# Mix and branch products with the tokens standing still and 512 weight columns moving

## The chip, the cores and the metric

The kernel runs on one core of a Trainium2 chip. The time is device time in microseconds of one execution; lower is better. Three timed runs of the kernel before gave 646.74, 647.31 and 647.63 us, and their median is what the change is compared with.

The engines have short names here. PE is TensorE, which multiplies; PEld is its loading of the operand that stands still. DVE is VectorE, ACT is ScalarE, POOL is GpSimd, and SP starts the loads. A product (one MATMUL) holds a 128x128 block in the array and moves up to 512 columns of the other operand past it. The block that stands still is loaded by an LDWEIGHTS instruction of its own, one for each product.

## The reference

Two layers are computed on 256 tokens of 1024 features. Each layer projects the normed tokens (w_in), runs three attentions (branches a, b and m), and merges the three results with gates that come from a "mix" projection:

```python
    ys = jnp.stack([ya, yb, ym], axis=2)
    up = jnp.einsum('bsnw,nwd->bsnd', ys, w_branch)
    gates = jax.nn.sigmoid(mix.reshape(b, s, N_BRANCH, D_MODEL))
    merged = jnp.sum(gates * up, axis=2)
    return x + jnp.einsum('bsd,de->bse', merged, w_out)
```

The mix projection has 3 x 1024 columns of w_in with 1024 rows each. The branch product has 3 x 512 rows and 1024 columns. The merged matrix, 256 x 1024, goes through w_out. After the second layer the tokens are normed once more and written out.

## The kernel before

All products are in float32, with each operand split in a high and a low part (`split`, lines 101 to 103: ACT rounds the value to `hi`, DVE subtracts to get `lo`). A product of the computation is then three products on the engine (`mm3`, lines 105 to 108: high by high, high by low, low by high).

Weights come in units (`unit`, lines 78 to 90): one load of up to 128x1024 float32 into `raw`, then the split into `whi` and `wlo`. There are four buffers of each, so PE can be at most four units behind the load.

Two helpers do the projections. `rows_first` (line 160) holds 128 tokens still and moves up to 512 weight columns; its result has tokens on partitions. `cols_first` (line 178) holds 128 weight columns still and moves all 256 tokens; its result has the columns on partitions. The queries, keys and values use `rows_first`; the gates and the mix use `cols_first`.

At the end of each layer the merge runs over eight blocks of 128 merged columns. `mixes(j)` (lines 510 to 519) projects block j of the three branches and takes tanh of half of it on ACT. The loop over j (lines 525 to 549) does the branch products of block j, 36 of 256 columns each, into two PSUM banks (`ups`). DVE forms (tanh + 1) * up for the three branches (line 543), POOL adds the three (lines 545 and 546), ACT writes half the sum to `mh[:, j]` (line 547) and DVE the rest to `ml[:, j]` (line 548). Since the columns are on partitions there, `mh` and `ml` are already in the form that `w_out` holds still. `mixes` runs three blocks ahead of the merge.

Then `w_out` multiplies: for k from 0 to 7 it takes block k of `mh` and `ml` against row block k of w_out, 12 products of 512 columns for each k. In the second layer the last three k stand behind the loop, and one bank's columns are cut in two.

A scheduler sets the order of the instructions on each engine when the kernel is built. It moves instructions past one another where the data allow it, and each engine then works off its own list strictly in order. So the mix products stand partly among the attention of branch b, where PE would otherwise wait for softmax.

Of the kernel before, what the change touches and what calls it, by code (L numbers as in the profile page):

```python
# [13 lines left out]
P = 128  # L14
# [11 lines left out]
RAW = 4  # units of weights on their way  # L26
WARM = 10  # products on zeros that wake the tensor engine's clock while the first loads are under way
WS = (64 ** -0.5) * (8 ** -0.5)

# columns of w_in, in groups of 512  # L30
# [4 lines left out]
def trunk(ctx, tc, x, x_t, mem, mem_t, consts, norm_g, gains, w_grp, w_idx, w_mix, w_kv, w_br, w_o, final_g, out):  # L35
# [13 lines left out]
    def two(tag="big"):  # L49
        """a tile for the high and the low parts: [P, 2, 1024]"""  # L50
        return big.tile([P, 2, 1024], F32R, tag="big", name=tag)
# [43 lines left out]
    def load_after(dst, src):  # L95
        """a load that waits for the newest unit, so that it doesn't hold up the units before it"""
        nc.gpsimd.tensor_copy(dst.rearrange("p a b -> p (a b)")[:, 0:1] if len(dst.shape) > 2 else dst[:, 0:1],
                              newest[0][:, 0:1].bitcast(F32))
        nc.sync.dma_start(dst, src)
# [19 lines left out]
    def transpose_to(dst_fn, src, t):  # L119
        """[P, 1024] -> 8 blocks [128, P]; dst_fn(c, psum [P, 4, 128])"""  # L120
# [6 lines left out]
    def rstd_row(rows, rs):  # L127
        """1 / rms of the tokens: on partitions in rs, and in a row, the same on all partitions"""
# [11 lines left out]
    def mem_prep(l, mh, ml, ks):  # L140
        """mem but for 1 / rms, with features on partitions"""
# [18 lines left out]
    def rows_first(wsrc, xh, xl, parts, n, done, ahead=lambda u: None, pools=None, first=False):  # L160
        """tokens on partitions: out[t][:, part] = x @ w, w [P, KC, n]"""
# [16 lines left out]
    def cols_first(wsrc, xh, xl, nt, done, ahead=lambda u: None):  # L178
        """columns on partitions: out[c] = (x @ w).T, w [P, KC, nt * 128]; done(pair of tiles, psum)"""
# [16 lines left out]
    def rope(t, ps, dst, nh):  # L196
        """dst [P, nh, 64] = rope of psum [P, nh, 64]"""
# [11 lines left out]
    def heads_T(qf, dst):  # L209
        """qf[t] [P, 512] -> dst [P, 2, (pair, token)], heads on partitions"""  # L210
# [18 lines left out]
    def values(l, g, hh, hl, name):  # L229
        """[P, token tile, (head, part, 64)]: the high part first for even heads, last for odd ones, so that it  # L230
        meets the rows of y that the head has"""
# [10 lines left out]
    def gate(l, g, hh, hl, s2):  # L242
        """s2 [P, 4, S] = 2 silu(h @ w).T"""
# [6 lines left out]
    def probs(t, nk, tm, nb, scale=-1.0):  # L250
        """softmax rows of scale * tm, whose maximum is -nb"""
# [11 lines left out]
    def pair_scores(p, qT, kT, at):  # L263
        """both heads of a pair, each on its half of the rows and in its own bank: queries of the first tile
        meet the high and the low parts of their 128 keys side by side, those of the second tile all keys"""
# [30 lines left out]
    def attn_out(p, prs, v, y, s2):  # L296
# [13 lines left out]
        for i, pool in enumerate(((psa, "sc"), (pst, "pt"))):  # L310
            # high and low parts of v on rows; the low parts of the second queries' later keys in columns of their own
# [59 lines left out]
    def index_mask(l, hh, hl):  # L371
        """additive masks of the keys that each query picks"""
# [39 lines left out]
        def turn(t, r):  # L412
            """one turn of a query tile: takes the 8 largest that are left, the earlier of equals first"""
# [16 lines left out]
    def normed_first(xT):  # L430
        """of x that is laid out with features on partitions"""
# [23 lines left out]
    for l in range(L):  # L455
# [54 lines left out]
        def mixes(j):  # L510
            """tanh(mix / 2).T of columns j of the branches"""
            mx = wk.tile([P, 3, S], F32, tag="mix", name="mx", bufs=5)

            def done(c, ps):
                n = 2 if c == 0 else 1
                nc.scalar.activation(mx[:, 2 * c:2 * c + n, :], ps[:, :n * S].rearrange("p (a b) -> p a b", b=S),  # L516
                                     AF.Tanh, scale=0.5)
            cols_first(w_mix[l, j], hh, hl, 3, done)
            return mx

# [3 lines left out]
        mxs = [mixes(j) for j in range(3)]  # L524
        for j in range(8):
            if j + 3 < 8:
                mxs.append(mixes(j + 3))
            if j == 4 and l + 1 < L:
                mhl = mem_tiles()
                mem_prep(l + 1, *mhl, range(KC))  # L530
            ups = [bank(pmm, "mm"), bank(pmm, "mm")]
            for u in range(2):
                hi, lo = unit(w_br[l, j, :, u * 6:(u + 1) * 6, :], 768)
                for q in range(6):
                    n, k = divmod(u * 6 + q, 4)
                    o = ups[n // 2][:, (n % 2) * S:(n % 2 + 1) * S]
                    ww = slice(q * P, (q + 1) * P)
                    yy = slice(k * S, (k + 1) * S)
                    mm3(o, hi[:, ww], lo[:, ww], ys[n][:, 0, yy], ys[n][:, 1, yy], k == 0 and n != 1, k == 3)
            mx = mxs[j]  # L540
            mt = [mx[:, n, :] for n in range(3)]
            for n in range(3):
                nc.vector.scalar_tensor_tensor(mt[n], mx[:, n, :], 1.0, ups[n // 2][:, (n % 2) * S:(n % 2 + 1) * S],  # L543
                                               op0=ALU.add, op1=ALU.mult)
            nc.gpsimd.tensor_tensor(mt[0], mt[0], mt[1], op=ALU.add)  # L545
            nc.gpsimd.tensor_tensor(mt[0], mt[0], mt[2], op=ALU.add)  # L546
            nc.scalar.activation(mh[:, j, :], mt[0], AF.Copy, scale=0.5)  # L547
            nc.vector.scalar_tensor_tensor(ml[:, j, :], mt[0], 0.5, mh[:, j, :].bitcast(F32),
                                           op0=ALU.mult, op1=ALU.subtract)
# [124 lines left out]
```

## Time and profile before

| what | value |
|---|---|
| median of three runs | 647.31 us |
| lowest and highest | 646.74 and 647.63 us |
| span of the profiled execution, first to last instruction | 645.5 us |
| PE busy | 632.1 us, 98% of the span, 4446 recorded products |
| DVE busy | 468.8 us, 73% |
| ACT busy | 372.6 us, 58% |
| POOL busy | 121.0 us, 19% |
| read from memory | 106.81 MB, 167 GB/s over the span |

The profile gives the span of its execution as its time; the median of the timed runs lies 1.8 us above it. Busy time says that an engine had at least one instruction in work. Since products overlap in the array (one is recorded for 0.28 to 0.40 us, the next begins 0.12 to 0.23 us later), the price of a product is read from the distance between two starts, not from its recorded length.

### The profile page before, as it was taken

The numbers are of one execution on the slowest core, as the hardware profiler recorded it, in microseconds if no ns is written. First come the engines' busy times: TensorE is split into PE (matmuls) and PEld (weight loads), VectorE is DVE, ScalarE is ACT, GpSimd is POOL, SyncE is SP. The second block draws the span as 40 slices with busy tenths as digits, with TensorE's granted clock in tenths as the row PEclk, the third lists the DMA queues.
The fourth block names the chain that finished last, engine by engine and source line by source line (L and its number), as shares of the span: only waits on it lengthen the run. The fifth ranks groups of instructions, "written<-read, shape, count | busy, mean of one in ns | idle before, by whom it ended". The sixth has DMA issues, their size and how long they took to land.

```text
span 645.5 us, 12071 instructions
## 1 busy us (share of the span) xinstructions
PE 632.1 (98%) x4446; PEld 583.1 (90%) x4446; DVE 468.8 (73%) x1014; ACT 372.6 (58%) x725; POOL 121.0 (19%) x182
## 2 busy tenths in 40 slices
PE   7999999999999999999999999999999999999995
PEld 4989889878999999999889998897898999999984
DVE  5678799778777778557584678987777786755763
ACT  5857655666656756444464656656565766544442
POOL 1303022023102302126010200401210211221422
PEclk9999999999999999999999999999999999999998
DMA  8967454454444456667655745445444445566641
GB/s 298 360 201 233 150 160 141 156 162 137 111 142 124 125 145 198 195 174 221 214 174 135 264 152 164 134 133 170 151 127 133 131 127 148 171 187 184 206 127 65
DMA packets 35051, 108.64 MB, mean 168 GB/s; under 512 B 4016, under 2 KB 4016, under 8 KB 34992
## 3 DMA queue, kind: packets, MB, share of 16 engines
q1 hardware_dynamic: 34704, 107.35, 54.7%
q8 instruction: 35, 0.57, 0.4%
q10 hardware_dynamic: 288, 0.52, 0.2%
q14 instruction: 24, 0.20, 0.1%
HBM read 106.81 MB, written 1.05 MB: 167 GB/s over the span
## 4 chain that ended last, share of the span: by engine, by line
PE 93%; DMA 3%; DVE 2%; ACT 1%; issue 1%; SPq 0%; POOLq 0%; POOL 0%; ACTq 0%; DVEq 0%
PE mm L106 24%; PE mm L108 24%; PE mm L107 24%; PE sc L271 2%; PE sc L108 2%; PE sc L106 2%; PE sc L107 2%; DMA raw<-in_w_kv 2%; PE sc L275 2%; PE pt L216 1%; PE pt L301 1%; DMA xT<-in_x_t 1%; PE pt L106 1%; PE pt L108 1%; PE pt L107 1%; PE pt L303 1%
## 5 line engine op out<-in xcount | busy, mean ns | idle before, releaser
L103 DVE TENSOR_TENSOR wlo<-raw,whi 128x1024 fp32r<-128x1024 f32 (+3 forms) x225 | 246.9, 1099 | 99.5 <-ACT whi L102 98.5
L102 ACT CAST whi<-raw 128x1024 fp32r<-128x1024 f32 (+3 forms) x225 | 208.1, 927 | 130.3 <-PE mm L107 52.0
L107 PE MATMUL mm<-hl,whi 128*128 128x256 f32 x640 | 183.4, 287 | 0.0
L106 PE MATMUL mm<-hh,whi 128*128 128x256 f32 x640 | 182.9, 286 | 0.0
L108 PE MATMUL mm<-hh,wlo 128*128 128x256 f32 x640 | 182.6, 286 | 0.0
L106 PEld LDWEIGHTS mm<-hh,whi 128*128 128x128 f32 x640 | 122.6, 192 | 1.3
L107 PEld LDWEIGHTS mm<-hl,whi 128*128 128x128 f32 x640 | 122.6, 192 | 0.8
L108 PEld LDWEIGHTS mm<-hh,wlo 128*128 128x128 f32 x640 | 122.4, 192 | 0.7
L108 PE MATMUL mm<-whi,hl 128*128 128x512 f32 (+1 forms) x224 | 84.8, 381 | 1.4 <-DVE hl L103 1.4
L107 PE MATMUL mm<-wlo,hh 128*128 128x512 f32 (+1 forms) x224 | 85.7, 384 | 0.0
L106 PE MATMUL mm<-whi,hh 128*128 128x512 f32 (+1 forms) x224 | 84.2, 380 | 0.0
L260 POOL TENSOR_SCALAR pr<-pr,rinv 128x256 f32<-128x256 f32 (+1 forms) x80 | 40.7, 526 | 183.6 <-DVE rinv L258 175.9
L108 PEld LDWEIGHTS mm<-whi,hl 128*128 128x128 f32 x224 | 42.1, 189 | 8.3 <-DVE hl L103 1.7
L107 PEld LDWEIGHTS mm<-wlo,hh 128*128 128x128 f32 x224 | 42.2, 189 | 7.0
L106 PEld LDWEIGHTS mm<-whi,hh 128*128 128x128 f32 x224 | 41.8, 188 | 7.3
L255 ACT ACTIVATE pr<-tm,nb 128x128 f32<-128x128 f32 (+1 forms) x80 | 36.5, 459 | 9.1 <-DVE nb L291 9.0
L545 POOL TENSOR_TENSOR mx<-mx 128x256 f32<-128x256 f32 x16 | 21.3, 1334 | 102.8 <-DVE mx L543 102.8
L207 POOL TENSOR_TENSOR qf<-rt,rt 128x128 f32<-128x128 f32 (+2 forms) x24 | 16.8, 704 | 121.2 <-DVE rt L206 121.2
L546 POOL TENSOR_TENSOR mx<-mx 128x256 f32<-128x256 f32 x16 | 23.1, 1446 | 12.6 <-DVE mx L543 11.5
L543 DVE SCALAR_TENSOR_TENSOR mx<-mx,mm 128x256 f32<-128x256 f32 x48 | 18.6, 415 | 6.6 <-PE mm L108 6.5
L516 ACT ACTIVATE mx<-mm 128x512 f32<-128x512 f32 (+1 forms) x32 | 15.7, 490 | 12.9 <-PE mm L108 12.9
L547 ACT ACTIVATE mgh<-mx 128x256 fp32r<-128x256 f32 x16 | 6.7, 418 | 25.5 <-POOL mx L546 25.5
(252 smaller groups left out, 1220.9 us busy)
## 6 DMA issues: line engine op xcount, KB each, us to landing
raw<-in_w_grp SPq DMA_DIRECT2D x80, 512.0 KB, 3.9
raw<-in_w_mix SPq DMA_DIRECT2D x64, 384.0 KB, 3.2
raw<-in_w_br SPq DMA_DIRECT2D x32, 384.0 KB, 3.4
raw<-in_w_o SPq DMA_DIRECT2D x16, 512.0 KB, 4.4
raw<-in_w_kv SPq DMA_DIRECT2D x15, 512.0 KB, 4.4
raw<-in_w_idx SPq DMA_DIRECT2D x16, 292.0 KB, 3.1
memT<-in_mem_t SPq DMA_DIRECT2D x4, 256.0 KB, 6.0
xr<-in_x SPq DMA_DIRECT2D x2, 512.0 KB, 6.6
```

Of the source, the lines that this page charges most:

```text
L102: nc.scalar.copy(hi, src)
L103: nc.vector.tensor_sub(lo, src, hi.bitcast(F32))
L106: nc.tensor.matmul(o, lh, rh, start=start, stop=False, skip_group_check=True)
L107: nc.tensor.matmul(o, lh, rl, start=False, stop=False, skip_group_check=True)
L108: nc.tensor.matmul(o, ll, rh, start=False, stop=stop, skip_group_check=True)
L207: nc.gpsimd.tensor_tensor(dst[:, :, 0:16], t1[:, :nh], t2[:, :nh], op=ALU.add)
L255: nc.scalar.activation(pr[:, i, :nk], tm[:, i, :nk], AF.Exp, bias=nb[:, i:i + 1], scale=scale, accum_out=rsum[:, i:i + 1])
L260: nc.gpsimd.tensor_scalar(pr[:, i, :nk], pr[:, i, :nk], rinv[:, i:i + 1], 1.0, op0=ALU.mult, op1=ALU.mult)
L516: nc.scalar.activation(mx[:, 2 * c:2 * c + n, :], ps[:, :n * S].rearrange("p (a b) -> p a b", b=S), AF.Tanh, scale=0.5)
L543: nc.vector.scalar_tensor_tensor(mt[n], mx[:, n, :], 1.0, ups[n // 2][:, (n % 2) * S:(n % 2 + 1) * S], op0=ALU.add, op1=ALU.mult)
L545: nc.gpsimd.tensor_tensor(mt[0], mt[0], mt[1], op=ALU.add)
L546: nc.gpsimd.tensor_tensor(mt[0], mt[0], mt[2], op=ALU.add)
```

## The change

The mix projection and the branch products take 512 weight columns at a time with the tokens still, so that their results have tokens on partitions. The merge runs over two halves b of 512 merged columns and three branches n, in six steps instead of eight. `mixes(b, n)` is now a `rows_first` with two banks, one for each 128 tokens, and one tanh for each. `merge(b, n)` does the branch products of one branch, 24 of 512 columns, multiplies them on DVE by (tanh + 1), and from the second branch on adds the result to the first branch's on POOL. After the third branch `merged_T` transposes the 128x512 halves on PE, four 128x128 blocks for each 128 tokens, and ACT and DVE write `mh` and `ml` from the transposed bank. The arrays w_mix and w_br are laid out for this on the host. `w_out` is unchanged.

```diff
-        def mixes(j):
-            """tanh(mix / 2).T of columns j of the branches"""
-            mx = wk.tile([P, 3, S], F32, tag="mix", name="mx", bufs=5)
...
-            cols_first(w_mix[l, j], hh, hl, 3, done)
+        def mixes(b, n):
+
+            mx = wk.tile([P, NT, 512], F32, tag="mix", name="mx", bufs=4)
+            rows_first(w_mix[l, b, n], hh, hl, [(0, 512)], 512,
+                       lambda t, i, ps: nc.scalar.activation(mx[:, t], ps, AF.Tanh, scale=0.5))
             return mx
+
+        def merge(b, n, mx, acc):
+
+            ups = [bank(pmm, "mm") for _ in range(NT)]
+            for u in range(2):
+                hi, lo = unit(w_br[l, b, n, :, 2 * u:2 * u + 2, :], 1024)
+                for q in range(2):
+                    k = 2 * u + q
+                    ww = slice(q * 512, (q + 1) * 512)
+                    for t in range(NT):
+                        yy = slice(k * S + t * P, k * S + (t + 1) * P)
+                        mm3(ups[t], ys[n][:, 0, yy], ys[n][:, 1, yy], hi[:, ww], lo[:, ww], k == 0, k == 3)
+            for t in range(NT):
+                nc.vector.scalar_tensor_tensor(mx[:, t], mx[:, t], 1.0, ups[t], op0=ALU.add, op1=ALU.mult)
+                if n:
+                    nc.gpsimd.tensor_tensor(acc[:, t], acc[:, t], mx[:, t], op=ALU.add)
+
+        def merged_T(b, acc):
+
+            bs = slice(4 * b, 4 * b + 4)
+            for t in range(NT):
+                tt = slice(t * P, (t + 1) * P)
+                pt = bank(pmm, "mm")
+                for i in range(4):
+                    nc.tensor.transpose(pt[:, i * P:(i + 1) * P], acc[:, t, i * P:(i + 1) * P], ident)
+                pt = pt.rearrange("p (a b) -> p a b", b=P)
+                nc.scalar.activation(mh[:, bs, tt], pt, AF.Copy, scale=0.5)
+                nc.vector.scalar_tensor_tensor(ml[:, bs, tt], pt, 0.5, mh[:, bs, tt].bitcast(F32),
+                                               op0=ALU.mult, op1=ALU.subtract)
...
-        mxs = [mixes(j) for j in range(3)]
-        for j in range(8):
-            if j + 3 < 8:
-                mxs.append(mixes(j + 3))
-            if j == 4 and l + 1 < L:
+        todo = [(b, n) for b in range(2) for n in range(3)]
+        mxs = [mixes(*todo[j]) for j in range(3)]
+        for j, (b, n) in enumerate(todo):
+            if j == 3 and l + 1 < L:
                 mhl = mem_tiles()
                 mem_prep(l + 1, *mhl, range(KC))
...
+            merge(b, n, mxs[j], mxs[3 * b])
+            if j + 3 < 6:
+                mxs.append(mixes(*todo[j + 3]))
+            if n == 2:
+                merged_T(b, mxs[3 * b])
```

The names in the rows below: `hh` and `hl` are the normed tokens, `yA`, `yM`, `yB` the branch results, `mm`, `sc` and `pt` PSUM banks, `mx` the tanh and then the gated branches, `mgh` and `mgl` the tiles that the code calls mh and ml, `cst` holds the identity. A line that begins with a minus stands in the list of before alone, one with a plus in that of after alone, one with neither in both.

PE in the first layer, among the last projections of the attention of branch b, where the first mix products stand:

```order
+L107 MATMUL mm<-wlo,hh 128x512
+L108 MATMUL mm<-whi,hl 128x512
+L106 MATMUL mm<-whi,hh 128x512
 L216 MATMUL pt<-cst,qf 128x128 x4
-L107 MATMUL mm<-hl,whi 128x256
 L271 MATMUL sc<-bk,bq 128x256 x4
 L275 MATMUL sc<-bk,bq 128x256 x6
-L108 MATMUL mm<-hh,wlo 128x256
-L106 MATMUL mm<-hh,whi 128x256
```

Each pair of 256-column products there has become one of 512 columns, in which the tokens (`hh`, `hl`) stand still; the attention's own products have stayed where they were among them.

PE at the end of the first layer's merge, before: the branch products run straight into those of w_out.

```order
L106 MATMUL mm<-yB,whi 128x256
L107 MATMUL mm<-yB,whi 128x256
L108 MATMUL mm<-yB,wlo 128x256
L106 MATMUL sc<-whi,mgh 128x512
L107 MATMUL sc<-wlo,mgh 128x512
L108 MATMUL sc<-whi,mgl 128x512
L106 MATMUL pt<-whi,mgh 128x512
```

PE at the same place after, where the products of w_out for k = 2 are under way:

```order
L106 MATMUL pt<-whi,mgh 128x512
L107 MATMUL pt<-wlo,mgh 128x512
L540 MATMUL mm<-cst,mx 128x128 x4
L108 MATMUL pt<-whi,mgl 128x512
L106 MATMUL sc<-whi,mgh 128x512
L540 MATMUL mm<-cst,mx 128x128 x4
L107 MATMUL sc<-wlo,mgh 128x512
```

The transposes of the second half now stand among the w_out products, 26 products behind the last branch product in the first layer (27 in the second), and the second four come two products later (three in the second layer). Those of the first half stand together, eight in a row, behind the last mix product.

DVE at the end of the first layer's merge, after, with the engines that each instruction waits for:

```order
L529 SCALAR_TENSOR_TENSOR mx<-mx,mm 128x512 [waits PE_49,Pool_49]
L103 TENSOR_TENSOR wlo<-raw,whi 128x1024 [waits DMAHW2_49,Activation_49]
L529 SCALAR_TENSOR_TENSOR mx<-mx,mm 128x512 [waits PE_49]
L103 TENSOR_TENSOR wlo<-raw,whi 128x1024 [waits DMAHW3_49,Activation_49]
L103 TENSOR_TENSOR wlo<-raw,whi 128x1024 [waits DMAHW4_49,Activation_49]
L529 SCALAR_TENSOR_TENSOR mx<-mx,mm 128x512 [waits PE_49,Pool_49]
L529 SCALAR_TENSOR_TENSOR mx<-mx,mm 128x512 [waits PE_49]
L103 TENSOR_TENSOR wlo<-raw,whi 128x1024 [waits DMAHW5_49,Activation_49]
```

Before, three half as wide ones stood between two splits there, with the write of `mgl` ahead of them. Now the two multiplications of the last branch stand behind the splits of the first three w_out units, and POOL's last two adds wait for them.

## Rows read from the trace of the kernel before

**Rows 1.** The page: engine, busy us, share of the span, instructions.

```profile
PE 632.1 (98%) x4446; PEld 583.1 (90%) x4446; DVE 468.8 (73%) x1014; ACT 372.6 (58%) x725; POOL 121.0 (19%) x182
```

**Rows 2.** The page: the chain that ended last, by engine.

```profile
PE 93%; DMA 3%; DVE 2%; ACT 1%; issue 1%; SPq 0%; POOLq 0%; POOL 0%; ACTq 0%; DVEq 0%
```

**Rows 3.** Stretches: us, busy PE, PEld, DVE, ACT, POOL, granted clock, DMA, GB/s.

```profile
130.00:140.00 10.00, 10.00 (x54) 7.98 (x54) 8.38 (x24) 6.40 (x17) 3.27 (x8) 1.00 0.54 161
...
240.00:250.00 10.00, 10.00 (x86) 10.00 (x85) 8.59 (x17) 7.72 (x16) 1.32 (x1) 1.00 0.64 193
...
270.00:280.00 10.00, 10.00 (x86) 10.00 (x85) 5.51 (x9) 4.88 (x8) 2.77 (x2) 1.00 0.69 181
...
310.00:320.00 10.00, 10.00 (x46) 8.29 (x45) 4.10 (x4) 4.21 (x4) 0.00 (x0) 1.00 0.70 224
```

**Rows 4.** All waits of PE: who for whom, us, times, longest.

```profile
PE mm L106 <- ACT whi L102: 2.1, 2, 1.2
PE pt L74 <- POOL idle L71: 1.5, 1, 1.5
PE mm L108 <- DVE hl L103: 1.4, 1, 1.4
PE mm L107 <- DVE wlo L103: 0.5, 1, 0.5
```

**Rows 5.** PE, 262 to 282 us, mix and branch products: first, last of 169.

```profile
261.74 0.28 PE L107 MATMUL mm<-yB,whi 128*128 128x256 f32 x1
...
281.90 0.28 PE L107 MATMUL mm<-hl,whi 128*128 128x256 f32 x1
```

**Rows 6.** PE, 306 to 330 us, products of 512 columns: first, last of 107.

```profile
305.82 0.39 PE L108 MATMUL pt<-whi,mgl 128*128 128x512 f32 x1
...
329.85 0.39 PE L106 MATMUL mm<-whi,mh 128*128 128x512 f32 x1
```

**Rows 7.** PE around eight transposes: start us, recorded us, line, operation.

```profile
332.35 0.40 PE L108 MATMUL mm<-whi,ml 128*128 128x512 f32 x1
332.58 1.04 PE L124 MATMUL pt<-cst,h 128*128 128x128 f32 x8
333.37 0.48 PE L106 MATMUL mm<-whi,mh 128*128 128x512 f32 x1
333.69 0.40 PE L107 MATMUL mm<-wlo,mh 128*128 128x512 f32 x1
```

**Rows 8.** Groups by form: line, engine, operation, count, busy us, mean ns, idle before.

```profile
L103 DVE TENSOR_TENSOR wlo<-raw,whi 128x1024 fp32r<-128x1024 f32 x111 | 138.1, 1245 | 49.2 <-ACT whi L102 48.4
...
L102 ACT CAST whi<-raw 128x1024 fp32r<-128x1024 f32 x111 | 116.4, 1050 | 71.0 <-PE mm L108 19.8 <-issue 16.3 <-PE mm L107 10.6
...
L247 DVE SCALAR_TENSOR_TENSOR s<-th,mm 128x512 f32<-128x512 f32 x12 | 8.2, 685 | 1.1 <-ACT th L246 1.0
...
L145 DVE SCALAR_TENSOR_TENSOR ml<-memT,gm,mh 128x256 fp32r<-128x256 f32 x16 | 6.8, 478 | 5.2 <-ACT mh L144 5.2
...
L362 DVE SCALAR_TENSOR_TENSOR pl<-pt,rsm,ph 128x512 fp32r<-128x512 f32 x8 | 5.7, 737 | 0.0
```

**Rows 9.** POOL's adds: count, shortest, median, longest ns, first and last start.

```profile
L545 POOL TENSOR_TENSOR mx<-mx x16: 737/1358/1592, 237.2 to 616.0; 128x256 f32<-128x256 f32 x16
L546 POOL TENSOR_TENSOR mx<-mx x16: 1317/1442/1602, 243.7 to 617.6; 128x256 f32<-128x256 f32 x16
...
L589 POOL TENSOR_TENSOR o<-xr,gb x1: 1276/1276/1276, 637.2 to 637.2; 128x512 f32<-128x512 f32 x1
```

More of the change, by code (lines that the diff above doesn't have):

```diff
@@ L508, in trunk @@
         attend(bq, bk, lambda: values(l, B_V, hh, hl, "bv"), masks, yB, s2[1])
-        def mixes(j):
-            mx = wk.tile([P, 3, S], F32, tag="mix", name="mx", bufs=5)
[L514 to L517, printed above, removed]
-            cols_first(w_mix[l, j], hh, hl, 3, done)
-            return mx
+        def mixes(b, n):
+            mx = wk.tile([P, NT, 512], F32, tag="mix", name="mx", bufs=4)
+            rows_first(w_mix[l, b, n], hh, hl, [(0, 512)], 512,
+                       lambda t, i, ps: nc.scalar.activation(mx[:, t], ps, AF.Tanh, scale=0.5))
+            return mx
+        def merge(b, n, mx, acc):
[23 more added lines that the diff above has]
+                                               op0=ALU.mult, op1=ALU.subtract)
         mh = big.tile([P, KC, S], F32R, tag="big", name="mgh")
@@ L523, in trunk @@
         ys = [yA, yM, yB]
-        mxs = [mixes(j) for j in range(3)]
-        for j in range(8):
-            if j + 3 < 8:
-                mxs.append(mixes(j + 3))
-            if j == 4 and l + 1 < L:
+        todo = [(b, n) for b in range(2) for n in range(3)]
+        mxs = [mixes(*todo[j]) for j in range(3)]
+        for j, (b, n) in enumerate(todo):
+            if j == 3 and l + 1 < L:
                 mhl = mem_tiles()
                 mem_prep(l + 1, *mhl, range(KC))
[L531 to L549, printed above, removed]
+            merge(b, n, mxs[j], mxs[3 * b])
[3 more added lines that the diff above has]
+                merged_T(b, mxs[3 * b])
         last = 3 if l + 1 == L else 0
@@ L645 @@
     order = [0, 2, 1]
-    mix = wr[..., 5704:].reshape(L, P, KC, 3, 8, P)[:, :, :, order]
-    mix = mix.transpose(0, 4, 1, 2, 3, 5).reshape(L, 8, P, KC, 384)
-    br = w_branch[:, order].reshape(L, 3, 4, P, 8, P).transpose(0, 4, 3, 1, 2, 5).reshape(L, 8, P, 12, P)
+    mix = wr[..., 5704:].reshape(L, P, KC, 3, 2, 512)[:, :, :, order].transpose(0, 4, 3, 1, 2, 5)
+    br = w_branch[:, order].reshape(L, 3, 4, P, 2, 512).transpose(0, 4, 1, 3, 2, 5)
     arrays = {
```

## The prediction, made before the changed kernel ran

> **What bounds the kernel now.** I read the page's busy times first, then its chain, then the stretches. PE is busy for 98% of the span while DVE, at 73%, is next [rows 1]. That alone says little, since a product is recorded for longer than it occupies the array. The chain is the better witness: 93% of what ended last is PE's own work [rows 2]. In the stretches PE is busy for the whole 10 us, in the attention (130 to 140 us), in the mix and branch products (240 to 280 us) and in w_out (310 to 320 us), at a granted clock of 1.00, the 2.4 GHz level [rows 3]. All of PE's waits together are 5.5 us, and none is for a gated branch, for POOL's adds or for `mgl` [rows 4]. So in the stage that changes PE is the bound, DVE and ACT have 14 to 51% left, and a change is worth there what it takes from PE's list or adds to it.
>
> **What one product costs.** It is read between starts. In the mix and branch stage 169 products of 256 columns begin between 261.74 and 281.90 us: 20.16 / 168 = 0.1200 us each [rows 5]. In w_out and the memory projection 107 products of 512 columns begin between 305.82 and 329.85 us: 24.03 / 106 = 0.2267 us each [rows 6]. Two narrow products take 0.2400 us, a wide one 0.2267, for the same arithmetic. If each product is a part per column plus a fixed part, the fixed part is 0.0133 us, and the change removes one for each pair. In all 107 the weights move and tokens or merged columns stand still, as in the new products, so the wide price is that of the new form.
>
> **Products removed and added.** Before, one layer has 8 blocks x 24 column tiles (8 row blocks x 3 branches) x 3 = 576 mix products and 8 x 36 = 288 branch products, 864 in all; two layers have 1728 of 256 columns. They go, and 864 of 512 columns come. 1728 x 0.1200 = 207.4 us become 864 x 0.2267 = 195.9 us: 11.5 us less on PE.
>
> At this place a rule speaks against the change. The Trainium skill, "TensorE: Matmul & The Clock Gate", section "Back-to-back issue gap", gives N / 2.4 + 2.5 ns between starts at full clock. An estimate by it would be 109.2 and 215.8 ns, 2.6 ns saved per pair and 2.2 us in all, less than the transposes below cost. The trace does not agree: both prices are higher [rows 5, 6], and the saving per pair is 13.3 ns.
>
> **Transposes added.** Four blocks for each 128 tokens, each half and each layer: 32. Around eight of them the product before starts at 332.35 and the second product after at 333.69 us [rows 7]; of the 1.34 us two normal spacings (0.45) are the products' own, so eight cost 0.89 us, of which 0.10 is the hand-over behind them. Each layer has one group of eight and two of four (half of 0.79 plus 0.10, so 0.49): 2 x (0.89 + 0.98) = 3.7 us on PE.
>
> **Work beside PE.** A unit of 1024 columns takes 1.25 us on DVE and 1.05 on ACT [rows 8] and feeds 12 wide products, 2.72 us of PE, in the mix as in the branches. The same helper feeds the same widths in w_out today, where PE has no hole [rows 3]. So splits and loads stay hidden. The tanh, the gating and the writing of `mgh` and `mgl` become fewer and wider; on an engine with idle time that is worth nothing. Mix products also fill PE among the softmax of branch b. There the narrow ones are replaced by wide ones, as branch a has them today without a hole at 130 to 140 us [rows 3]. I take nothing for that; bounds 0 and 1.5 us, the latter the size that the totals of PE's waits have [rows 4].
>
> **The new wait.** Before, the merged blocks left the branch products one by one, and only the last of eight was young when w_out needed it, seven blocks later. Now the second half's transposes stand in PE's list behind POOL's last adds, and everything behind them on PE waits too. In the first layer 26 w_out products cover that (5.9 us from the last branch product, which I call E), and the second four follow at E + 5.9 + 0.49 + 2 x 0.227 = E + 6.8. In the second layer it is 27, and E + 7.3.
>
> What must be done by then, first layer: from the start of the half's first branch product to E PE has 75 products, 17.0 us. In that time DVE has six splits (7.5 us), two writes of `mgl` (1.5), eight preparations of the next layer's memory (3.8) and six gatings (4.1) [rows 8], 16.9 us; it starts about 1 us late, behind two tanh and a cast on ACT, so its last gating ends near E + 1.1. POOL has four adds in a row, from the first gating of the middle branch (by the same walk E - 4.8). With a for one 128x512 add they end at E - 4.8 + 4a, and PE stands still for 4a - 11.6 us if that is positive. In the second layer the memory is not prepared; the adds start near E - 5.1, and the loss is 4a - 12.4.
>
> No row has this add at this place. The bound below is 1.28 us, the one 128x512 add, at the end where DVE does little [rows 9]. The bound above is twice the longest half-wide add, 2 x 1.60 = 3.20; twice the medians is 2.7 to 2.9. At 2.9 both losses are nil, at 3.20 they are 1.2 and 0.4 us. I take nothing, by the medians, and keep 0 to 1.6 us. After the transposes ACT and DVE need about 0.7 us each per 128 tokens [rows 8], with 19 products (4.3 us) of k = 2 and 3 left on PE in the first layer; that is covered. The first half's transposes have 48 mix products (10.9 us) in front of them, more than a gating and two adds at 3.20. If any of this cover were missing, a whole chain of gating, add, transpose and two writes would cost at most 0.7 + 2 x 3.2 + 0.5 + 1.4 = 9.0 us per layer.
>
> **The sum.** -11.5 + 3.7 + 0 = -7.8 us. The profiled span of 645.5 becomes 637.7. The median lies 1.8 us above that span, so the time is 639.5 us.
>
> **Rivals.**
> - *Part of it is given back* (0.09). The adds take 3.2 us or more, or DVE, which the first layer's second half leaves with hardly any slack, comes late, or PE finds holes among the softmax of branch b. For it: DVE's 16.9 us against PE's 17.0. Against it: PE waited for none of these before [rows 4]. Price 2 to 6.5 us: 641.5 to 646.
> - *The adds become the bound, slower than before* (0.04). One mechanism at one place: POOL's four adds before the second half's transposes. The loss over both layers is 8a - 24.0 us; it eats the gain at a = 4.0, and the kernel is slower by more than 0.2% from a = 4.1. At a = 4.5 it is 12.0 us and the time 651.5. For it: the half-wide add goes from 0.74 to 1.60 us within this kernel [rows 9], so something stretches it up to twofold. Against it: 4.0 would be 2.5 times the longest of the 32.
> - *The change does not do what it says: the wide product saves nothing in this place* (0.03). Then only the transposes are left, +3.7 us, 651.0. Against it: the same form, tokens still and 512 columns, runs in the attention's projections at no visible loss, and 0.2267 is measured in the stage right behind [rows 6]. The rule of the skill named above would give 2.2 us back, -2.2 + 3.7 = +1.5 us, 648.8, a milder form of this rival.
>
> **How the numbers follow.** The forecast, a saving of some 6 to 9 us, has 0.84: 638.5 to 641.5, which are the two unknowns' bounds (1.6 and 1.5 us less than fully added) and half a microsecond of spread, as in the three runs. The range for 8 in 10 reaches a little into the first rival: 638.3 to 643.5. A measurement of this kernel can tell about 0.2%, 1.3 us, from no change, so faster means below 646.0. Forecast and nearly all of the first rival lie there, 0.91; same 0.04; slower 0.05, from the last two rivals with a little of each left in between.
>
> **What would show it.** Right, step by step: starts in the mix and branch products 0.227 us apart; 1728 fewer and 864 + 32 more products; eight transposes taking about 0.8 us; no wait of PE for POOL's adds or only tenths; PE busy through every stretch from 130 us on; 128x512 adds between 1.3 and 3.2 us. Wrong: a wait of PE at the transposes of the second half, several microseconds long, would be the second rival; waits for `whi` and `wlo` in the branch products of the first layer's second half, the first; a spacing near 0.240, the third.

## The result, and the profile after

The changed kernel takes 640.54 us, the median of 4 runs (640.47 to 640.62), against 647.24 us (646.74 to 647.63) for the kernel before on the same chip. The ratio is 0.9896, 95% interval 0.9882 to 0.991: faster by 6.7 us. The forecast was 639.5, so the time lies inside the range, 1.0 us above the forecast. The profiled execution spans 638.7 us (645.5 before).

The page of the kernel after, its engines and its chain, to be read beside [rows 1, 2]:

```profile
PE 626.2 (98%) x3614; PEld 540.2 (85%) x3614; DVE 467.3 (73%) x958; ACT 368.9 (58%) x685; POOL 105.5 (17%) x166
...
PE 94%; DVE 2%; DMA 1%; issue 1%; ACT 0%; POOLq 0%; SPq 0%; POOL 0%; ACTq 0%; DVEq 0%
```

PE has 832 instructions fewer, which is 1728 less 864 less 32. It still makes up nearly the whole chain, so what leaves PE's list leaves the time.

Two of the stretches of [rows 3], after (from and to, length, then busy us and instructions of PE, PEld, DVE, ACT and POOL, granted clock, DMA share, GB/s):

```profile
240.00:250.00 10.00, 10.00 (x50) 8.32 (x49) 5.32 (x7) 5.97 (x10) 0.00 (x0) 1.00 0.59 187
270.00:280.00 10.00, 10.00 (x46) 8.29 (x45) 5.61 (x6) 4.15 (x4) 3.54 (x2) 1.00 0.61 204
```

PE is busy throughout at a granted clock of 1.00, with about half as many products. It is so in the other two stretches too, 130 to 140 and 310 to 320 us. All of its waits, as in [rows 4]:

```profile
PE mm L106 <- ACT whi L102: 1.6, 1, 1.6
PE pt L74 <- POOL idle L71: 1.5, 1, 1.5
PE mm L108 <- DVE hl L103: 1.4, 1, 1.4
PE mm L108 <- DVE wlo L103: 0.2, 1, 0.2
```

None is for POOL's adds, for a gating or for `mgl`, and all four lie before 180 us. The new price of a product, in a run of products with nothing between them (first and last of 23; start us, recorded us, engine, line, operation):

```profile
283.78 0.39 PE L107 MATMUL mm<-wlo,yA 128*128 128x512 f32 x1
...
288.76 0.39 PE L108 MATMUL mm<-whi,yM 128*128 128x512 f32 x1
```

4.98 / 22 = 0.2264 us, the spacing of w_out in [rows 6].

**Where the time came from.** Two marks are the same work in both kernels: the first transpose of branch b's queries, which stands just ahead of what the change touches in the first layer, and the first transpose of the next layer's norm, which stands behind it (its row of before is in [rows 7]). Before, the first mark:

```profile
178.66 0.49 PE L216 MATMUL pt<-cst,qf 128*128 128x128 f32 x3
```

After, both marks:

```profile
178.98 0.49 PE L216 MATMUL pt<-cst,qf 128*128 128x128 f32 x3
...
329.38 0.49 PE L124 MATMUL pt<-cst,h 128*128 128x128 f32 x3
```

From mark to mark it was 153.92 us and is 150.40: 3.52 less. The start is 0.32 later. From the second mark to the last product PE needs 304.75 us before (637.33 - 332.58) and 301.19 after: 3.56 less. 0.32 - 3.52 - 3.56 = -6.76, the 6.8 us between the spans.

The stretch between the marks, by kind of product. Each column sums the distances from one start to the next, so a hand-over is counted with the neighbour in which it falls; each entry is rounded by itself. The last two columns belong to experiments below.

| us between the marks (count) | before | after | e1, 256 | e3, no transposes |
|---|---|---|---|---|
| products of 256 columns | 105.78 (864) | none | 105.63 (864) | none |
| products of 512 columns | 37.20 (163) | 137.14 (595) | 37.43 (163) | 136.80 (595) |
| transposes of the merged matrix | none | 1.50 (16) | 1.50 (16) | none |
| transposes of probabilities (24) | 1.56 | 2.00 | 1.56 | 2.00 |
| transposes of queries and keys (16) | 1.50 | 1.67 | 1.50 | 1.67 |
| probabilities times values (24) | 2.96 | 3.18 | 3.20 | 3.18 |
| scores (40) | 4.92 | 4.90 | 4.92 | 4.90 |
| sum | 153.92 | 150.40 | 155.73 | 148.56 |

### The profile page after: what moved, and what is told of

It is laid out like the page before. It is cut to its first block, busy times and chain, and to the rows that moved or that the text cites. A ratio compares the mean times of both kernels' runs of the same rounds, so it can differ in the third digit from the quotient of the medians.

```text
span 638.7 us, 10185 instructions
## 1 busy us (share of the span) xinstructions
PE 626.2 (98%) x3614; PEld 540.2 (85%) x3614; DVE 467.3 (73%) x958; ACT 368.9 (58%) x685; POOL 105.5 (17%) x166
## 3 DMA queue, kind: packets, MB, share of 16 engines
HBM read 106.81 MB, written 1.05 MB: 169 GB/s over the span
## 4 chain that ended last, share of the span: by engine, by line
PE 94%; DVE 2%; DMA 1%; issue 1%; ACT 0%; POOLq 0%; SPq 0%; POOL 0%; ACTq 0%; DVEq 0%
PE mm L107 25%; PE mm L108 25%; PE mm L106 25%; PE sc L271 2%; PE sc L106 2%; PE sc L107 2%; PE sc L108 2%; PE sc L275 2%; PE pt L216 1%; PE pt L301 1%; PE pt L106 1%; PE pt L107 1%; PE pt L108 1%; DMA raw<-in_w_grp 1%; PE pt L303 1%; DMA memT<-in_mem_t 1%
## 5 line engine op out<-in xcount | busy, mean ns | idle before, releaser
L103 DVE TENSOR_TENSOR wlo<-raw,whi 128x1024 fp32r<-128x1024 f32 (+2 forms) x201 | 246.4, 1229 | 109.9 <-ACT whi L102 108.9
L102 ACT CAST whi<-raw 128x1024 fp32r<-128x1024 f32 (+2 forms) x201 | 204.2, 1018 | 151.5 <-PE mm L108 67.3
L108 PE MATMUL mm<-whi,hl 128*128 128x512 f32 (+2 forms) x416 | 160.3, 387 | 1.4 <-DVE hl L103 1.4
L107 PE MATMUL mm<-wlo,hh 128*128 128x512 f32 (+2 forms) x416 | 160.8, 387 | 0.0
L106 PE MATMUL mm<-whi,hh 128*128 128x512 f32 (+2 forms) x416 | 159.7, 386 | 0.0
L108 PE MATMUL mm<-hh,wlo 128*128 128x256 f32 x256 | 73.3, 287 | 0.2 <-DVE wlo L103 0.2
L107 PE MATMUL mm<-hl,whi 128*128 128x256 f32 x256 | 73.3, 287 | 0.0
L106 PE MATMUL mm<-hh,whi 128*128 128x256 f32 x256 | 72.7, 285 | 0.0
L106 PEld LDWEIGHTS mm<-hh,whi 128*128 128x128 f32 x256 | 48.9, 191 | 0.4
L107 PEld LDWEIGHTS mm<-hl,whi 128*128 128x128 f32 x256 | 48.9, 191 | 0.4
L514 ACT ACTIVATE mx<-mm 128x512 f32<-128x512 f32 x24 | 14.1, 596 | 12.0 <-PE mm L108 11.5
```

The lines of the kernel that those rows point to most:

```text
L102: nc.scalar.copy(hi, src)
L103: nc.vector.tensor_sub(lo, src, hi.bitcast(F32))
L106: nc.tensor.matmul(o, lh, rh, start=start, stop=False, skip_group_check=True)
L107: nc.tensor.matmul(o, lh, rl, start=False, stop=False, skip_group_check=True)
L108: nc.tensor.matmul(o, ll, rh, start=False, stop=stop, skip_group_check=True)
L514: lambda t, i, ps: nc.scalar.activation(mx[:, t], ps, AF.Tanh, scale=0.5))
```

## The experiments

The theory: each product costs a fixed 13.3 ns beside its columns, PE's list is the time, the transposes take their forecast price, and POOL's adds end before PE needs them. The rivals: the gain came from something else in the new arrangement than the width; the transposes or the adds cost a different sum than they seem to. Each ratio below is against the kernel before timed beside the run (medians 647.03 to 647.26 us); differences to the changed kernel go by its 640.54 us, so some 0.2 us of them may be no more than the spread of these medians.

**e9, the changed kernel again.** It gives the noise of a second look. Nothing is edited.

> The changed kernel once more. The first transposes of the branch b queries began at 178.98 us in its first trace and at 178.66 in that of the kernel before, with nothing but loads, stores and the same products ahead of them in both. If that 0.32 us is chance in the first loads, it will be another value here, within about 1 us, while the stretch from there to the next layer's first transposes keeps its 150.4 us. If the change causes it, it comes out at 178.98 again.

Measured: 640.67 us (640.49 to 640.89), ratio to before 0.9896 (0.9881 to 0.9911). Its first mark stands at 179.00 us and its second at 329.39, within 0.02 us of the first look, so the changed kernel's start repeats. Of the kernel before there is one trace only, and the spans of its other timed executions run from 644.5 to 646.1 us: whether the 0.3 us is the program's or that one execution's isn't shown.

**e1, the new arrangement with products of 256 columns.** Tokens still stand and the transposes stay; each product of the mix and of the branches is cut in two, so only the width is undone. Both places are cut alike:

```
-mm3(ups[t], ys[n][:, 0, yy], ys[n][:, 1, yy], hi[:, ww], lo[:, ww], k == 0, k == 3)
+for c, d in [(0, 256), (256, 512)]:
+    mm3(ups[t][:, c:d], ys[n][:, 0, yy], ys[n][:, 1, yy], hi[:, q * 512 + c:q * 512 + d],
+        lo[:, q * 512 + c:q * 512 + d], k == 0 and c == 0, k == 3)
```

> Tokens still as in the changed kernel, same units, same transposes, but each product of 512 weight columns in the mix and branch products is cut in two of 256. My theory (PE is the bound, and a product pays a fixed part of 13.3 ns however wide it is): the 864 fixed parts come back, 864 x 0.0133 = 11.5 us, so 640.5 + 11.5 = 652.0 us, slower than the kernel before by the transposes; starts 0.120 us apart. Rival (the gain came from what else changed: 72 wide units a layer pair less in loads and splits, wider work on ACT and DVE, another order): the cut changes nothing and the time stays at 640.5. Third, on the third of a microsecond per layer that the profiled run lacks against the prediction: if the attention's small products cost more because wide products stand next to them, the starts behind the transposes of lines 301 and 303 come back from about 81 ns to the 56 to 74 ns of the kernel before.

Measured: 650.24 us (650.02 to 650.45), ratio 1.0048 (1.0032 to 1.0065): the gain is gone and a loss stands in its place. PE in e1's mix products, first and last of 19:

```profile
257.83 0.28 PE L108 MATMUL mm<-whi,hl 128*128 128x256 f32 x1
...
259.99 0.28 PE L108 MATMUL mm<-whi,hl 128*128 128x256 f32 x1
```

2.16 / 18 = 0.1200 us, the price of [rows 5], with tokens standing instead of weights: at this width it doesn't matter which operand stands. Between the marks e1 takes 155.73 us, 5.33 more than the changed kernel, or 12.3 ns for each of 432 cuts. Twice that is 10.7; its first mark comes 1.1 us earlier (177.86), so that about the 9.7 us measured are left, where two prices of 0.1200 for one of 0.2267 would be 11.5. What the fixed part consists of stays open: a product less is a weight load less too, in every run here.

**e2, cut at 384 instead.** The same edit with (0, 384) and (384, 512): as many products as in e1, with unequal widths.

> As the run before, but each product of 512 columns is cut in one of 384 and one of 128. If a product costs a fixed part and a part per column (0.4167 ns, from 0.1200 and 0.2267 us at 256 and 512), it makes no difference where the cut lies: 652.0 us, as with 256 and 256. Rival: a narrow product is held up by the loading of its own standing block, which takes about as long as the spacing of the transposes of 128 columns, 0.099 us; then the 128-column product costs 0.099 instead of 0.067 us, and the time is 652.0 + 864 x 0.032 = 680 us.

Measured: 691.57 us (691.08 to 693.04), ratio 1.069 (1.0674 to 1.0706). A sum of columns and a fixed part should have given e1's time, so that sum doesn't hold for the products of 128 columns. PE in e2's mix:

```profile
258.06 0.39 PE L106 MATMUL mm<-whi,hh 128*128 128x384 f32 x1
258.29 0.34 PE L107 MATMUL mm<-wlo,hh 128*128 128x384 f32 x1
258.47 0.34 PE L108 MATMUL mm<-whi,hl 128*128 128x384 f32 x1
258.64 0.22 PE L106 MATMUL mm<-whi,hh 128*128 128x128 f32 x1
258.70 0.27 PE L107 MATMUL mm<-wlo,hh 128*128 128x128 f32 x1
258.81 0.27 PE L108 MATMUL mm<-whi,hl 128*128 128x128 f32 x1
258.92 0.40 PE L106 MATMUL mm<-whi,hh 128*128 128x384 f32 x1
```

PE's weight loads beside them:

```profile
258.64 0.19 PEld L107 LDWEIGHTS mm<-wlo,hh 128*128 128x128 f32 x1
258.75 0.19 PEld L108 LDWEIGHTS mm<-whi,hl 128*128 128x128 f32 x1
258.86 0.19 PEld L106 LDWEIGHTS mm<-whi,hh 128*128 128x128 f32 x1
```

Three of 384 and three of 128 take 0.86 us, 0.287 per pair instead of 0.2267 for one wide product; 0.060 x 864 pairs = 52 us, and the measured difference to the changed kernel is 51. From one product of 384 columns to the next it is 0.17 to 0.18 us, which still is the columns and 13 ns (0.173). Around the products of 128 columns starts are 0.11 us apart, and so are the loads of the next standing block, each product following its load by 0.06 us. So these products seem to wait for their blocks: two limits, of which the later one decides, and at 256 columns the columns with their 13 ns still do. The Trainium skill, "TensorE: Matmul & The Clock Gate", section "LDWEIGHTS (loading the stationary operand)", gives P / 1.2 ns for P columns, by which an estimate for 128 is 107 ns; the 0.11 us agree.

**e3, no transposes.** The merged matrix goes to the output product as it is, so the output isn't that of the kernel; four lines become one:

```
-pt = bank(pmm, "mm")
-for i in range(4):
-    nc.tensor.transpose(pt[:, i * P:(i + 1) * P], acc[:, t, i * P:(i + 1) * P], ident)
-pt = pt.rearrange("p (a b) -> p a b", b=P)
+pt = acc[:, t].rearrange("p (a b) -> p a b", b=P)
```

> The 32 transposes are left out: mgh and mgl are written straight from the gated sums with tokens on partitions, so w_out multiplies an untransposed matrix; nothing else is changed. My theory: PE is the bound there too, and all 32 are paid for, 16 starts of 93 ns per layer plus three hand-overs of 0.1 us: 3.0 to 3.7 us less, 636.8 to 637.5 us. Rival: they stand in time that PE would otherwise spend waiting for POOL's adds: the time stays within 0.5 us of 640.5.

Measured: 636.89 us (636.01 to 637.27), ratio 0.9839 (0.9825 to 0.9854): 3.65 us below the changed kernel. Between the marks 1.84 us are gone, the 1.50 of the transposes and 0.34 of hand-overs, counted with the products beside them.

**e5 and e6, POOL's adds twice and three times.** Each add is issued two or three times, so that the output is another; everything else stays in the code:

```
-nc.gpsimd.tensor_tensor(acc[:, t], acc[:, t], mx[:, t], op=ALU.add)
+for _ in range(2):
+    nc.gpsimd.tensor_tensor(acc[:, t], acc[:, t], mx[:, t], op=ALU.add)
```

> Every add of POOL in the merge is issued twice (so the second and third branch count twice in the sum); the built order puts the second half's transposes 11 to 13 products further back for it. In the changed kernel's trace POOL's last adds end 2.8 us (first layer) and 1.9 us (second) before the second four transposes begin. My theory (a chain of gating and adds that costs nothing until it outlasts the w_out products ahead of the transposes): with 1.8 to 2.2 us for one add the four single adds become eight and end 0 to 3 us behind their new place in each layer, so 640.5 to 646 us, most likely 641.5. Rival (POOL's adds are spare work that PE never meets): 640.5. Second rival (every microsecond of the adds is on the path): the 30 us that all adds take are added, 670 us.

> As the run before, with each add three times (second and third branch count three times). The transposes of the second half now stand behind all 48 products of k = 0 to 3, and nothing more can be put before them. By my chain the twelve adds of a half end 5 to 9 us behind that place in each layer, and about 1 us behind the first half's: 652 to 662 us, PE waiting for POOL at the transposes. Rival (spare work): 640.5.

Measured: twice 642.98 us (642.79 to 643.75), ratio 0.9937 (0.9924 to 0.9951), 2.4 above the changed kernel; three times 660.07 (658.53 to 660.73), ratio 1.0196 (1.0182 to 1.021), 19.5 above. PE at the first layer's second half in e5 (in brackets the idle time before and who ended it); these two waits, 1.6 us, are all that e5 has for POOL's adds:

```profile
307.21 0.66 PE L541 MATMUL mm<-cst,mx 128*128 128x128 f32 x4 [0.49 <-POOL mx L532]
309.42 0.66 PE L541 MATMUL mm<-cst,mx 128*128 128x128 f32 x4 [1.08 <-POOL mx L532]
```

The same place, then the wait, in e6:

```profile
315.67 1.12 PE L541 MATMUL mm<-cst,mx 128*128 128x128 f32 x4 [4.24 <-POOL mx L532]
318.24 1.12 PE L541 MATMUL mm<-cst,mx 128*128 128x128 f32 x4 [1.46 <-POOL mx L532]
```

```profile
PE mm L541 <- POOL mx L532: 12.0, 8, 4.2
```

So the second rival's mechanism exists, at the place where it was put, and the kernel's own adds, half as many as e5's, end ahead of PE's need. Two reservations. With more adds the scheduler set the transposes further back among the w_out products: PE reaches the first four 9.0 us behind the last branch product in e5 and 5.9 in the changed kernel, of which only 0.49 is waiting. The runs therefore price longer adds with an adapted list, and not the point at which a fixed list would lose. And the 12.0 us of waiting aren't all of e6's loss. Two stretches of e6, the first with these waits, the second right behind it (columns as above):

```profile
312.00:318.00 6.00, 1.12 (x4) 0.72 (x4) 2.50 (x2) 1.11 (x2) 5.92 (x5) 0.76 0.64 198
318.00:324.00 6.00, 5.76 (x20) 4.81 (x21) 0.84 (x2) 0.60 (x1) 0.19 (x1) 0.67 0.00 0
```

PE was busy for 1.12 of 6 us, and the granted clock is 0.76 there and 0.67 in the next 6 us, where PE is busy again: these waits cost twice, once as idle time and once as a lower clock behind them.

**e4, the gates in the wide form too.** Each layer's three gate products take the same form: tokens stand, 512 columns move, eight transposes follow for each gate.

```
-cols_first(w_grp[l, g], hh, hl, 4, done)
+rows_first(w_grp[l, g], hh, hl, [(0, 512)], 512, done)
+for c in range(2):
+    ...
+            nc.tensor.transpose(pt[:, i * S + t * P:i * S + (t + 1) * P], gt[:, t, j * P:(j + 1) * P], ident)
+    nc.scalar.copy(s2[:, c * 512:(c + 1) * 512], pt)
```

> The changed kernel, and beside it the six gate projections (three in each layer) also with tokens still and 512 columns moving, gated there and then transposed in eight blocks each, with one more copy on ACT. By the same sum as for the merge, each of the six saves 48 fixed parts, 0.64 us, and adds eight transposes with two hand-overs, 0.99 us: 6 x 0.35 = 2.1 us more, 642.6 us. Rival (wide products are better whatever they cost elsewhere, or the transposes hide in waits): 640.5 - 3.8 = 636.7 us.

Measured: 645.56 us (644.92 to 646.73), ratio 0.9976 (0.9965 to 0.9987), 5.0 above the changed kernel; the sign is as expected, the size twice it. A gate needs 96 narrow products; 48 wide ones save 0.64 us (48 x 13.3 ns) and eight transposes cost about 0.9. The second layer loses 1.23 us, near the 1.05 worked out. The first loses 3.2, and in its index scores there (`sc<-ikT,iqT`, 40 products) PE takes 5.48 us instead of 3.57. PE among them:

```profile
77.31 0.38 PE L255 MATMUL pt<-cst,gt 128*128 128x128 f32 x2
77.44 0.48 PE L106 MATMUL mm<-whi,hh 128*128 128x512 f32 x1
77.76 0.39 PE L107 MATMUL mm<-wlo,hh 128*128 128x512 f32 x1
78.08 0.50 PE L279 MATMUL sc<-ikT,iqT 64*128 64x256 f32 x2
78.42 0.52 PE L283 MATMUL sc<-ikT,iqT 64*128 64x256 f32 x3
```

The scores stand in small groups between transposes and wide products, and starts around each change of kind are wider than within a run of one kind: 0.32 us from the first wide product to the second here, where a run has 0.227. That this is the whole of the extra 2 us isn't shown.

**e7 and e8, the same saving without transposes.** For the gates and the memory's queries the two halves `hh` and `hl` lie side by side, so that one `whi` block meets both in one product of 512 columns; `wlo` with `hh` stays at 256. Three products of 0.120 become one of 0.227 and one of 0.120. The two parts are then added on ACT and DVE. e7 keeps all four column blocks open at once, e8 runs in two passes over half the columns. The core of e7:

```
+nc.tensor.matmul(acc[c], hi[:, w], both, start=k == 0, stop=False, ...)
+nc.tensor.matmul(acc[c][:, :S], lo[:, w], both[:, :S], start=False, stop=k == KC - 1, ...)
...
+nc.scalar.copy(sm, acc[c][:, S:])
+nc.vector.tensor_add(sm, sm, acc[c][:, :S])
```

> The changed kernel with another way to save a product's fixed part, in the four projections of each layer that still hold the weights (the queries of branch m and three gates): the high and the low part of the tokens lie side by side, so that one product of 512 columns does high by high and high by low, and one of 256 does low by high. Nothing is transposed; the two halves of a bank are added on ACT and DVE at the end, and a projection takes four banks instead of two. By my theory each of the 256 triples costs 0.2267 + 0.1200 instead of 0.3600 us: 3.4 us less, 637.1 us. Rival: the four banks are all there are, and PE waits for their emptying between projections: up to 8 x 1 us lost, 640 to 645 us.

> As the run with the parts side by side, but each of the eight projections (queries of branch m and three gates, two layers) goes over its 512 columns in two passes of 256, so that it takes two banks at a time as before and the next pass finds two free. The units are laid out for it on the host and are as large and as many as before. My theory: the wide product of the two token parts costs 0.2267 and the narrow one 0.1200 us, and with the banks' wait gone 256 x 0.0133 = 3.4 us are saved against the changed kernel: 637.1 us. Rival: the loss lay not in the banks but in the added work on DVE and ACT (256 more columns to be copied and added for each block), which holds up the attention's chains: 640 us or more.

Measured: e7 651.45 us (649.62 to 652.76), ratio 1.0059 (1.0045 to 1.0072); e8 647.56 (646.16 to 649.29), ratio 1.0005 (0.9995 to 1.0015). Both lose to the changed kernel, by 10.9 and 7.0 us, though PE has 256 products fewer and the prices are the expected ones (0.230 and 0.120 between starts). PE's waits that are new in e7:

```profile
PE pt L235 <- DVE aq L104: 4.0, 2, 2.0
PE mm L206 <- DVE sm L212: 3.0, 2, 2.0
```

The second is the wait that e7's rival named, for a bank that DVE has yet to read. And in e8:

```profile
PE pt L238 <- DVE aq L104: 3.4, 2, 1.7
PE mm L107 <- DVE sm L215: 1.6, 2, 0.8
```

In both, PE's transposes of branch a's queries wait until DVE has split the queries before them, and e8 still waits for banks. That the added sums on DVE cause the first wait isn't shown: until then e8 has eight of them (3.3 us, all before 75 us), but DVE's index search, which stands ahead of the split, also ends 8 us later than in the changed kernel (its last `MATCH_REPLACE8` starts at 115.96 instead of 107.94 us). In e8 the distances from these transposes to the next starts add up to 4.63 us instead of 1.42 in the first layer and 4.64 instead of 1.42 in the second, waits included: 6.4 us of the 10.5 by which e8 misses 637.1. Most of the rest stands right behind the waits, where PE is slower for a while:

```profile
120.64 0.63 PE L109 MATMUL mm<-whi,hx 128*128 128x512 f32 x1
121.07 0.63 PE L107 MATMUL mm<-whi,hx 128*128 128x512 f32 x1
```

Products of 512 columns are 0.43 us apart there. The granted clock is 0.51 from 119.5 to 123.0 us and 0.50 from 433.6 to 437.0, the 1.2 GHz level, and PE was busy for 1.14 of the 3.5 us ahead of the first of these stretches. Their 8 and 9 products take 3.4 us more than at 0.2267. e7 has three such stretches at 0.50 (63.0 to 66.3, 124.3 to 127.7 and 438.4 to 441.8 us), each behind a wait of 2 us. So a wait of PE costs twice here too, as in e6. No version beat the changed kernel; e3, which is below it, computes less.

## Why the prediction came out as it did

**Products.** Right. The spacing is 0.2264 us against 0.2267 taken. Between the marks the products cost 142.98 us before and, without any merge transposes beside them (e3), 136.80: 6.18 less, where 5.75 was worked out per layer. Neither kind keeps its price throughout, since a product behind other work stands wider: the old ones cost 2.1 us more than 864 x 0.1200, the new ones 1.7 more than 432 x 0.2267, and the difference is the 0.43. e1 is the proof that the gain is the width's: with the width undone and all else kept, the time goes above the old one.

**The rule of the Trainium skill** ("TensorE: Matmul & The Clock Gate", section "Back-to-back issue gap", N / 2.4 + 2.5 ns, which the section gives for single products) would have made the kernel slower, 648.8 us by the estimate. Measured are 640.54 us, with 120.0 ns between starts in e1 and 226.4 in the changed kernel: for these operands the trace disagrees and decides.

**Transposes.** Right: 1.84 us per layer (e3 against after) for 1.87, in two layers 3.65 for 3.7. A group of eight costs what [rows 7] said. After, behind the first half's last mix product:

```profile
280.38 0.40 PE L108 MATMUL mm<-whi,hl 128*128 128x512 f32 x1
280.62 1.04 PE L540 MATMUL mm<-cst,mx 128*128 128x128 f32 x8
281.41 0.48 PE L106 MATMUL mm<-whi,yA 128*128 128x512 f32 x1
281.73 0.40 PE L107 MATMUL mm<-wlo,yA 128*128 128x512 f32 x1
```

1.35 less 0.45 is 0.90 us, where 0.89 was taken.

**The fill of the attention.** The term that was too small. "I take nothing for that; bounds 0 and 1.5 us" looked for holes of PE, and there are none. But the small products of branch b's attention that stand among the mix products take 0.82 us more in the first layer (11.76 against 10.94: transposes of probabilities +0.44, of queries and keys +0.17, probabilities times values +0.22, scores -0.02). The cost is in the spacing, not in waits. It isn't the width of the neighbours as such: two probability transposes from 225.62 us on take 0.14 us between wide products, and two at the same time of e1 take 0.14 between narrow ones. It is the order. With wide products, five groups of probability transposes stand directly behind scores and one group of queries directly ahead of them; before, and in e1, another product always stands between. A group of four, after and before:

```profile
209.02 0.50 PE L275 MATMUL sc<-bk,bq 64*128 64x256 f32 x2
209.44 0.66 PE L301 MATMUL pt<-cst,pr 128*128 128x128 f32 x4
209.86 0.48 PE L106 MATMUL mm<-whi,hh 128*128 128x512 f32 x1
```

```profile
205.45 0.60 PE L301 MATMUL pt<-cst,pr 128*128 128x128 f32 x4
205.81 0.37 PE L107 MATMUL mm<-hl,whi 128*128 128x256 f32 x1
```

0.42 against 0.36 us: five times 0.06 and 0.17 for the group ahead of scores are 0.46 of the 0.61. The other 0.16 is counting, because the 24 probability transposes form 11 groups instead of 13 and the hand-over behind a group is counted with the next product. e1 takes the order back, and with it the 0.61. The 0.22 of the probabilities times values stay in e1 (3.20), so that the width isn't their cause, and that cause is open.

**The new wait.** Right: PE doesn't wait for POOL. POOL's adds of the first layer's second half, and PE around them (the last branch product, then the second half's transposes):

```profile
292.75 4.44 POOL L531 TENSOR_TENSOR mx<-mx 128x512 f32<-128x512 f32 x2 [18.95 <-DVE mx L529]
299.02 3.53 POOL L531 TENSOR_TENSOR mx<-mx 128x512 f32<-128x512 f32 x2 [1.83 <-DVE mx L529]
```

```profile
298.28 0.39 PE L108 MATMUL mm<-whi,yB 128*128 128x512 f32 x1
...
304.41 0.60 PE L540 MATMUL mm<-cst,mx 128*128 128x128 f32 x4
...
305.31 0.60 PE L540 MATMUL mm<-cst,mx 128*128 128x128 f32 x4
```

E is 298.51. The second four transposes come at E + 6.8, as worked out, and the adds end at 302.55, 2.8 us ahead of them. In the second layer the second four come at E + 6.65, not at E + 7.3, since some of the w_out products ahead of them there are only 256 wide, and the rows leave 1.9 us (612.35 and 614.28). The four adds take 2.2, 2.3, 1.3 and 2.3 us, within the bounds 1.28 and 3.20 and under the 2.7 to 2.9 that the medians gave. The four adds weren't in a row: the first pair started at E - 5.8, a microsecond earlier than the walk had it, and POOL then stood idle for 1.83 us until DVE's last gatings. DVE's row for these:

```profile
298.20 1.27 DVE L529 SCALAR_TENSOR_TENSOR mx<-mx,mm 128x512 f32<-128x512 f32 x2
```

They end at 299.47, E + 1.0, where E + 1.1 was forecast. So the last link was the gating, and the adds behind it had time to spare.

**The sum.** Per layer, from the first: -6.18 + 1.84 + 0.82 = -3.52; forecast were -5.75 + 1.87 + 0 = -3.88. Two errors of opposite sign, 0.43 too little gain and 0.82 too little cost, leave 0.36 per layer with the 0.03 of the transposes. That they largely cancel is luck, and in part the same time counted on one side or the other, as in the 0.16 above; the net doesn't depend on that. Twice 0.36 and the 0.32 of the later start are 1.0 us: 638.7 for 637.7 in the span.

The start is open. It differs between programs: in e1, e2, e3, e5 and e6, which edit nothing ahead of it, the first mark lies between 177.86 (e1) and 179.42 us (e6). The step from span to time was right by luck. The 1.8 us were the distance of a median from another execution's span; run by run the times of the kernel before lie 2.1 to 2.2 us above their spans and those of the changed kernel 1.8, while the one traced span of before, 645.5, lies 0.4 above the median of its later spans (645.1). The account is good to a few tenths, and a forecast for this kernel can hardly be sharper.

**The rivals.** None came true. Part given back: no wait of PE, and 1.0 us instead of 2 to 6.5. Adds the bound: e6 shows what that would look like. The wide product saves nothing: 0.2264, not 0.240.

## What to carry to other kernels

Where TensorE is the chain, read the price of a product from distances between starts, at each width that the kernel holds, and count instructions: merging two products of 256 columns saves one fixed part, whichever operand stands. A transpose that pays for it must be shared: the merged matrix carries 432 merged pairs over 16 transposes per layer, while a gate has 48 over eight and loses. Put a term for the changes of kind in TensorE's list, and look which kinds come to stand next to each other in the new order. Look at the other engines' chains before adding work to them, since a wait of TensorE can also lower its clock behind it.

## What the runs showed that was not expected

- The sum of columns and a fixed part fails at 128 columns: after a product of 128 the next starts 0.11 us later, in step with the loads of the standing blocks, so 384 + 128 costs 0.287 us where 256 + 256 costs 0.240 (e2).
- Transposes cost the same between products of either width. Directly behind or ahead of the scores, of which a product takes 64 rows, they cost 0.06 to 0.17 us more for each group.
- POOL's add of 128x512 varies within one kernel. The group's row of after (count, shortest, median and longest ns, first and last start):

```profile
L531 POOL TENSOR_TENSOR mx<-mx x16: 1292/2240/2292, 254.5 to 610.1; 128x512 f32<-128x512 f32 x16
```

With 1.29 to 2.29 us in one place and the same size, a single row of another place ([rows 9], 1.276) was no more than its lower bound. There are two lengths rather than a spread: in this kernel all adds take 1.3 or 2.2 to 2.3 us. In e6 the ten adds during which DVE did nothing took 1.26 to 1.30 us, and in both kernels none of over 2 us ran with less than 1.1 us of one or two splits of DVE beside it. That they hold each other up wasn't tested.

- A wait of 4 us of TensorE brought the granted clock to 0.67 in the 6 us behind it (e6), and waits of 1.7 and 0.8 us shortly after each other brought it to 0.51 in the 3.5 us behind them (e8), while e5's waits of 0.5 and 1.1 us leave its mean clock at 0.997.
